# Gate columns inside wide products, bias rows on half the array, and a first block without lag in a four-layer hybrid network on one core

## The chip, the core and the metric

The kernel runs on one core of a Trainium2 chip. The metric is the device time of one execution in microseconds; before the change it is 2135.79 us, the median of three runs (2135.09 to 2136.02).

## What is computed

The reference sends one sequence of 256 positions, 1024 wide, through four layers. Each layer is a gated feed-forward block, a mixer and a second feed-forward block, each followed by a scaled residual and a layer norm. The mixers are, in order, a state-space mixer, attention with a forget gate ("fox"), attention over blocks ("moba", here one block, so plain causal attention), and a state-space mixer again. All is float32. Cut to what matters here:

```python
def mamba2_mixer(x, w_in, ...):
    zxbcdt = x @ w_in
    z, xbc, dt = jnp.split(zxbcdt, [SSM_D_INNER, SSM_D_INNER + SSM_CONV_DIM], axis=-1)
    ...
    dt = jax.nn.softplus(dt + dt_bias)

def fox_attention(x, w_in, b_f, w_out):
    q, k, v, f_logit = jnp.split(x @ w_in, [H * Dh, 2 * H * Dh, 3 * H * Dh], axis=-1)
    log_f = jax.nn.log_sigmoid(f_logit + b_f)
    cum = jnp.cumsum(log_f, axis=1)
    ...
    logits = einsum(qb, kb) * scale + (cq[..., :, None] - cum[..., None, :])
    p = jax.nn.softmax(jnp.where(kpos <= qpos, logits, -inf))
```

## The kernel before

The sequence is cut into two streams of 128 positions (`t` = 0 and 1), each a generator that receives one weight piece at a time. A piece is 1 MB: 128 partitions of 2048 columns. `fetch` loads it on SP's queue into one of three `raw` tiles; `load` splits it in four chunks into a high part `wh` (ScalarE, line 126) and the remainder `wl` (VectorE, line 127), five tiles each. Activations are split alike into `xh` and `xl` by `to_T`, after TensorE has transposed them (line 161, tile `tp`). Each product is three matmuls, `mm3` (lines 151 to 153): high by high, high by low, low by high. `proj512` covers half the contraction with a piece of 512 output columns, so two pieces make one bank; `proj256` covers all of it with 256 columns.

The planner at the end walks the blocks. Stream 0 takes piece `s`, then stream 1 takes piece `s - LAG`, with `LAG` = 2 and two pieces loaded ahead; at the end of a block stream 1 catches up. The tile scheduler then orders the instructions of each engine by priority and readiness; what is marked with `keep_in_program_order` stays where the code has it. PSUM has three pools of two banks: `T` (transposes, scores, small sums, tile `tp`), `G` (tile `gu`), and the accumulators (`acc`, `ga`).

The gates are separate. `small_w` loads and splits the 32 columns of dt (or the 16 of the forget gate) into the tile `dtw`, and `small_proj` (lines 324 to 334) multiplies them in 16 narrow matmuls per stream and layer. `log1p_exp` and the steps around it then turn them into log decays on VectorE; `stage_cum` sums them along the sequence with triangular matrices. In the fox layer `rows_T` (line 336) leaves the sums as rows, high parts on partitions 0 to 31 and low parts on 32 to 63, and `stage_s` adds each head's row to its scores with a full-array matmul whose moving operand is the 128 columns of one row tile and whose stationary operand is one column of the tile `sel` (line 649). A score block `stage_s` handles four heads of one stream: for each of two banks `Sv[0]`, `Sv[1]`, both from `T`, a mask product (line 644, tile `mlo`), the bias products, and then the score products on 64 partitions (line 655), which alternate between the two halves of the array in the code. Exponentials follow on ScalarE (line 663). The feed-forward activations are turned through DRAM by POOL's queue (lines 245 and 249, tiles `turn` and `aT`).

At the start, `init` loads stream 0's input, the first piece follows in four loads, then stream 1's input.

Of the kernel before, what the change touches and what calls it, by code (L numbers as in the profile page):

```python
# [7 lines left out]
F32 = mybir.dt.float32  # L8
# [7 lines left out]
D = 1024  # L16
# [23 lines left out]

SSM_ORDER = ["X0", "Z0", "X1", "Z1", "O0", "X2", "Z2", "X3", "O1", "Z3",
             "O2", "O3"]
ATT_ORDER = ["V0", "Q0", "V1", "Q1", "V2", "Q2", "V3", "Q3", "O0", "O1", "O2", "O3"]

# [5 lines left out]
def build(tc, x, wst, ln_g, ln_b, sm_dt, sm_rows, sm_conv, sm_nw, fx_f, fx_b, out, plan=None):  # L50
# [11 lines left out]
    if plan is None:  # L62
        plan = []
        for l in range(DEPTH):
            plan += [("ffn", l, 3 * l), ("mix", l, 3 * l + 1), ("ffn", l, 3 * l + 2)]

# [15 lines left out]
    nc.vector.memset(mhalf, -0.5)  # L82

    K = {}

    def consts():
# [13 lines left out]
        K["sel"] = cpool.tile([128, 32], FR, name="sel")  # L100
        nc.vector.tensor_add(K["sel"], ident[:, 0:32], ident[:, 32:64])
# [35 lines left out]
    def load(i, raw=None, pin=False):  # L137
# [20 lines left out]
    def transposes(src, n):  # L158
        tp = T()
        for j in range(n):  # L160
            nc.tensor.transpose(tp[:, j * 128:(j + 1) * 128], src[:, j * 128:(j + 1) * 128], ident)  # L161
        return tp

    def to_T(st, h):
        xh = spool.tile([128, KT, 128], FR, name=f"xh{st.t}", bufs=1)
        xl = spool.tile([128, KT, 128], FR, name=f"xl{st.t}", bufs=1)
        for half in range(2):
            tp = transposes(h[:, half * 512:half * 512 + 512], 4)
            sl = slice(half * 4, half * 4 + 4)
            split(tp.rearrange("p (a b) -> p a b", a=4), xh[:, sl], xl[:, sl])  # L170
# [153 lines left out]
    def small_proj(st, w, n, bias):  # L324

        ps = G()
        for k in range(KT):
            nc.tensor.matmul(ps[:, :2 * n], st.xh[:, k], w[:, k], start=k == 0, stop=False, skip_group_check=True)
            nc.tensor.matmul(ps[:, :n], st.xl[:, k], w[:, k, 0:n], start=False, stop=k == KT - 1,
                             skip_group_check=True)  # L330
        v = small()
        nc.vector.tensor_add(v[:, :n], ps[:, :n], bias)
        nc.vector.tensor_add(v[:, :n], v[:, :n], ps[:, n:2 * n])
        return v[:, :n]

# [10 lines left out]
    def sel(j):  # L346
        return bc(K["sel"][:, j:j + 1], 128)

    def small_w(src, n):
        raw = tmp(KT * n, "t1", 5)  # L350
        nc.sync.dma_start(raw, src)
        w = spool.tile([128, KT, 2 * n], FR, name="dtw", bufs=1)
        rv = raw.rearrange("p (k n) -> p k n", k=KT)
        split(rv, w[:, :, 0:n], w[:, :, n:2 * n])
        return w
# [6 lines left out]
    def ssm_small(j):  # L362
# [4 lines left out]
        s.dt = small_w(sm_dt[j], 32)  # L367
        s.rows = tmp(96, "rows", 1)
        nc.sync.dma_start(s.rows, bc(sm_rows[j:j + 1, :], 96))
# [3 lines left out]
        nc.scalar.activation(s.na, s.rows[:, 32:64], AF.Exp)  # L373
# [12 lines left out]
    def ssm(st, j):  # L386
# [4 lines left out]
        def stage_dt():  # L391
            v = small_proj(st, s.dt, 32, s.rows[:, :32])
# [49 lines left out]
        def stage_x(g):  # L442
            if t == 0:
                s.xb[g] = spool.tile([128, 6, S + 3], F32, name="xb", tag="t4", bufs=2)
                s.cv[g] = spool.tile([128, 6, S], F32, name="cv", tag="t4", bufs=2)
                nc.gpsimd.memset(s.xb[g][:, :, 0:3], 0.0)
            xc = tmp(512, "t2", 4)
            nc.scalar.activation(xc, bank.pop(g), AF.Copy)
            tp = transposes(xc, 4)
            nc.vector.tensor_copy(s.xb[g][:, 0:4, 3 + t * 128:131 + t * 128], tp.rearrange("p (a b) -> p a b", a=4))  # L450
# [3 lines left out]
        def stage_bc(g):  # L454
            bcs = tmp(256, "t1", 5)
            nc.scalar.activation(bcs, bank.pop(g)[:, :256], AF.Copy)
# [470 lines left out]
```

## Time and profile before

| | |
|---|---|
| median of three runs | 2135.79 us |
| profiled execution | 2134.62 us |
| its span | 2132.7 us |
| TensorE busy | 2108.4 us, 99% |
| VectorE, ScalarE, POOL busy | 69%, 55%, 22% |
| HBM traffic | 205 GB/s over the span |

A row of the timeline, as below, gives a start in us from the span's beginning, a duration, the engine, the line of the kernel, the operation, the output and input tiles and a count; a bracket tells the idle time before the instruction on its engine and what ended it. A matmul's duration contains its way through the array, which overlaps the next one, so the distance from start to start is what it takes of TensorE.

### The profile page before, as it was taken

How to read it: one execution, taken by the hardware profiler on the slowest of the kernel's cores; microseconds unless marked ns; L12 is line 12 of the kernel's file. 1: busy time of each engine (PE TensorE's matmuls, PEld its weight loads, DVE VectorE, ACT ScalarE, POOL GpSimd, SP SyncE). 2: the span in 40 equal slices, each digit the busy share in tenths (PEclk: the TensorE clock that was granted, in tenths of full speed). 3: DMA queues.
4: the chain of work that ended last, by engine and by line, in shares of the span. 5: the costliest groups of instructions: out<-in, count | busy, mean ns of one | idle time of the engine just before them, and what ended most of it. 6: DMA issues, size and time to landing. Idle time of an engine off the chain costs nothing.

```text
span 2132.7 us, 29860 instructions
## 1 busy us (share of the span) xinstructions
PE 2108.4 (99%) x10346; PEld 1745.6 (82%) x10346; DVE 1464.4 (69%) x2833; ACT 1172.6 (55%) x2446; POOL 474.0 (22%) x858
## 2 busy tenths in 40 slices
PE   8999999999999999999999999999999999999998
PEld 7888888888888888788888887788888888888886
DVE  6657888756766575755675575666575678898655
ACT  6445996544444555544544455544444448975442
POOL 2431000233143200043233300033323310002331
PEclk9999999999999999999999999999999999999999
DMA  9665554666576643466666653376666655546662
GB/s 318 226 228 200 179 197 160 225 230 224 199 254 227 222 159 119 155 233 222 221 226 231 229 200 131 129 247 219 225 225 232 223 198 201 179 167 217 232 228 94
DMA packets 225927, 438.81 MB, mean 206 GB/s; under 512 B 20464, under 2 KB 20976, under 8 KB 225776
## 3 DMA queue, kind: packets, MB, share of 16 engines
q1 hardware_dynamic: 197616, 394.92, 51.8%
q0 software_dynamic: 28160, 41.99, 6.6%
q8 instruction: 81, 1.33, 0.3%
q14 instruction: 70, 0.57, 0.1%
HBM read 414.74 MB, written 22.09 MB: 205 GB/s over the span
## 4 chain that ended last, share of the span: by engine, by line
PE 94%; DVE 2%; ACT 2%; DMA 1%; issue 1%; SPq 0%; POOL 0%; DVEq 0%; ACTq 0%
PE gu L151 16%; PE gu L153 16%; PE gu L152 16%; PE acc L153 9%; PE acc L151 9%; PE acc L152 9%; PE ga L151 4%; PE ga L152 4%; PE ga L153 4%; PE tp L161 3%; PE gu L513 1%; DVE wl L127 1%; PE gu L698 1%; ACT wh L126 1%; DMA raw<-in_w_dram 0%
## 5 line engine op out<-in xcount | busy, mean ns | idle before, releaser
L127 DVE TENSOR_TENSOR wl<-raw,wh 128x512 fp32r<-128x512 f32 x1408 | 887.5, 683 | 375.9 <-ACT wh L126 374.1
L126 ACT ACTIVATE wh<-raw 128x512 fp32r<-128x512 f32 x1408 | 776.4, 621 | 504.2 <-PE gu L153 225.0
L151 PE MATMUL gu<-wh,xh 128*128 128x512 f32 (+1 forms) x1600 | 618.9, 387 | 1.3 <-ACT t L522 1.2
L152 PE MATMUL gu<-wl,xh 128*128 128x512 f32 (+1 forms) x1600 | 617.9, 386 | 0.0
L153 PE MATMUL gu<-wh,xl 128*128 128x512 f32 (+1 forms) x1600 | 617.6, 386 | 0.0
L249 POOL DMA_DIRECT2D aT<-turn x640 | 348.3, 551 | 489.5 <-issue 301.1
L151 PE MATMUL acc<-wh,ah 128*128 128x512 f32 x896 | 352.8, 394 | 0.0
L153 PE MATMUL acc<-wh,al 128*128 128x512 f32 x896 | 352.3, 393 | 0.0
L151 PEld LDWEIGHTS gu<-wh,xh 128*128 128x128 f32 x1600 | 301.1, 188 | 62.3 <-ACT t L522 1.6
L152 PE MATMUL acc<-wl,ah 128*128 128x512 f32 x896 | 351.3, 392 | 0.0
L152 PEld LDWEIGHTS gu<-wl,xh 128*128 128x128 f32 x1600 | 301.1, 188 | 59.7 <-issue 0.5
L153 PEld LDWEIGHTS gu<-wh,xl 128*128 128x128 f32 x1600 | 300.9, 188 | 59.5 <-DVE xl L127 0.3
L273 ACT ACTIVATE t<-gu 128x256 f32<-128x256 f32 x176 | 67.5, 383 | 268.4 <-PE gu L153 247.8
L275 DVE TENSOR_TENSOR t<-t,gu 128x256 f32<-128x256 f32 x176 | 73.6, 418 | 193.3 <-ACT t L273 193.3
L153 PEld LDWEIGHTS acc<-wh,al 128*128 128x128 f32 x896 | 168.3, 188 | 36.3 <-DVE al L127 2.5
L151 PEld LDWEIGHTS acc<-wh,ah 128*128 128x128 f32 x896 | 168.3, 188 | 35.9 <-issue 1.5
L152 PEld LDWEIGHTS acc<-wl,ah 128*128 128x128 f32 x896 | 168.3, 188 | 34.5 <-issue 1.3
L245 POOL DMA_DIRECT2D turn<-tb x160 | 90.3, 565 | 328.3 <-DVE tb L243 305.0
L151 PE MATMUL ga<-wh,xh 128*128 128x512 f32 (+1 forms) x448 | 159.8, 357 | 1.4 <-ACT xh L126 1.4
L153 PE MATMUL ga<-wh,xl 128*128 128x512 f32 (+1 forms) x448 | 155.9, 349 | 0.0
L152 PE MATMUL ga<-wl,xh 128*128 128x512 f32 (+1 forms) x448 | 155.7, 348 | 0.0
L193 POOL TENSOR_TENSOR rstd<-ve,mhalf 128x1 f32<-128x1 f32 x24 | 22.6, 942 | 485.1 <-DVE ve L191 485.1
(171 smaller groups left out, 1667.9 us busy)
## 6 DMA issues: line engine op xcount, KB each, us to landing
raw<-in_w_dram SPq DMA_DIRECT2D x351, 1024.0 KB, 5.3
turn<-tb POOLq DMA_DIRECT2D x160, 128.0 KB, 3.2
aT<-turn POOLq DMA_DIRECT2D x640, 32.0 KB, 4.0
mt<-cums SPq DMA_DIRECT2D x32, 256.0 KB, 4.5
gb<-in_ln_g_dram SPq DMA_DIRECT2D x12, 512.0 KB, 4.8
gb<-in_ln_b_dram SPq DMA_DIRECT2D x12, 512.0 KB, 5.9
nw<-in_sm_nw_dram SPq DMA_DIRECT2D x8, 256.0 KB, 5.6
h<-in_x_dram SPq DMA_DIRECT2D x4, 256.0 KB, 4.2
```

Of the source, the lines that this page charges most:

```text
L126: a = nc.scalar.activation(wh, raw, AF.Copy)
L127: return a, nc.vector.tensor_sub(wl, raw, wh.bitcast(F32))
L151: nc.tensor.matmul(o, xh, wh, start=start, stop=False)
L152: nc.tensor.matmul(o, xh, wl, start=False, stop=False)
L153: nc.tensor.matmul(o, xl, wh, start=False, stop=stop)
L161: nc.tensor.transpose(tp[:, j * 128:(j + 1) * 128], src[:, j * 128:(j + 1) * 128], ident)
L193: nc.gpsimd.tensor_tensor(rstd, ve, mhalf, op=ALU.pow)
L245: nc.gpsimd.dma_start(dr, b.rearrange("p q k t -> p (q k t)"))
L249: nc.gpsimd.dma_start(aT[32 * q:32 * q + 32].rearrange("p i k t -> p i (k t)"), dv[q])
L273: nc.scalar.activation(sg, gu[:, :256], AF.Silu)
L275: nc.vector.tensor_mul(a, sg, gu[:, 256:])
L513: ins = nc.tensor.matmul(y[:, c64], mt[h // 4][:, h % 4], xd[:, c64], start=True, stop=True)
```

## The change

Four edits come together.

1. The dt columns join the first group's products: group 0's x, b and c columns and the 32 of dt (800 in all) become two banks of 416 and 384 columns in four pieces, which are padded to 2048 columns in memory and split only where they are filled (`cols`, `step`). The fox layer's 16 gate columns join the first value piece: 272 columns in two pieces. `small_w` and `small_proj` go. The order of stages in group 0 of the state-space layer follows: b, c and dt come with the first bank, x with the second.
2. The fox bias rows are written to DRAM and read back as a tile `biases` (`s.R`) of two halves of 64 partitions, by POOL's queue (`bias_rows`). One matmul on 64 partitions then adds the rows of one bank. The second score bank comes from `G`, and the first bias and score products keep their place.
3. The first scores of the fox layer come two pieces later (`wait`).
4. In the first block stream 1 runs without lag up to piece 6, with a lag of one up to 9, then two. Until piece 4 the TensorE products, transposes and splits keep the code's order (`opening`). A dummy SiLU stands at the start of ScalarE's work.

```diff
+        cols = [1664, 1664, 1536, 1536] if it == "X0" else [2048] * (3 if k == "X" else 2)
...
+        cols = [1088, 1088] if fox and it == "V0" else [2048] * (2 if k == "Q" else 1)
...
+    warm = cpool.tile([128, 1], F32, name="warm")
+    nc.scalar.activation(warm, mhalf, AF.Silu)
...
-        for c in range(0, 2048, 512):
-            sl = slice(c, c + 512)
+        step = cols[i] // (-(-cols[i] // 544))
+        for c in range(0, cols[i], step):
+            sl = slice(c, c + step)
...
+    opening = []
+
     def mm3(o, xh, xl, wh, wl, start, stop):
-        nc.tensor.matmul(o, xh, wh, start=start, stop=False)
+        first = nc.tensor.matmul(o, xh, wh, start=start, stop=False)
+        if opening:
+            tc.keep_in_program_order(first)
...
-    def proj512(st, ps, half, w):
+    def proj512(st, ps, half, w, n=512):
         wh, wl = w
         for kk in range(4):
             k = half * 4 + kk
-            mm3(ps, st.xh[:, k], st.xl[:, k], wh[:, kk * 512:(kk + 1) * 512], wl[:, kk * 512:(kk + 1) * 512],
+            mm3(ps[:, :n], st.xh[:, k], st.xl[:, k], wh[:, kk * n:(kk + 1) * n], wl[:, kk * n:(kk + 1) * n],
                 k == 0, k == KT - 1)
...
-    def small_proj(st, w, n, bias):
...
+    def bias_rows(c, dst):
+
+        dr = dpool.tile([2, 16, 128], FR, name="fbias", bufs=3)
+        for p in range(2):
+            nc.gpsimd.dma_start(dr[p], c[32 * p:32 * p + 16])
+        for b in range(2):
+            nc.gpsimd.dma_start(dst[64 * b:64 * b + 8], dr.rearrange("p (g i b) k -> b (p g) i k", g=4, i=2)[b])
...
         def stage_dt():
-            v = small_proj(st, s.dt, 32, s.rows[:, :32])
+            v = small()
+            nc.vector.tensor_add(v, bank["b"][:, 384:416], s.rows[:, :32])
...
         at(where["X", 0, 1], stage_dt)
-        at(where["X", 0, 2] + 1 - t, stage_cum)
+        at(where["X", 0, 3] + 1 - t, stage_cum)
         for g in range(N_GRP):
-            b = where["X", g, 2]
-            at(b - 1, stage_x, g)
-            at(b, stage_bc, g)
+            b = where["X", g, 2 if g else 3]
+            at(b - 1 if g else b, stage_x, g)
+            at(b if g else 1, stage_bc, g)
...
             def stage_cum():
-                d.rows = rows_T(d.h, d.l, K["ntri"], f"rowsT{t}")
+                own = rows_T(d.h, d.l, K["ntri"], "rowsT")
                 if t == 0:
-                    s.toend = rows_T(d.h, d.l, K["strict"], "rowsTe")
+                    R = spool.tile([128, 2, 384], FR, name="biases", tag="t4", bufs=2)
+                    nc.gpsimd.memset(R.bitcast(F32), 0.0)
+                    s.R = [R[:, :, 0:128], R[:, :, 128:384]]
+                    bias_rows(own, s.R[0])
+                    bias_rows(rows_T(d.h, d.l, K["strict"], "rowsTe"), s.R[1][:, :, 0:128])
+                else:
+                    bias_rows(own, s.R[1][:, :, 128:256])
...
-            Sv = [T()[:, :2 * nk].rearrange("p (h k) -> p h k", h=2) for b in range(2)]
+            Sv = [f()[:, :2 * nk].rearrange("p (h k) -> p h k", h=2) for f in (T, G)]
...
-                if fox:
-                    for i in range(2):
-                        for kt, off, rows in parts:
-                            nc.tensor.matmul(Sv[b][:, i, off:off + 128], sel(g * 4 + 2 * i + b), rows, start=False,
-                                             stop=True, skip_group_check=True)
+            halves = [slice(64 * b, 64 * b + 64) for b in range(2)]
+            if fox:
+                for b, half in enumerate(halves):
+                    ins = nc.tensor.matmul(Sv[b], K["sel"][half, g:g + 1].to_broadcast([64, 128]), s.R[t][half],
+                                           start=False, stop=True, skip_group_check=True)
+                    if b == 0:
+                        tc.keep_in_program_order(ins)
...
-            at(where["Q", 0, 0], stage_f)
-            at(where["Q", 0, 1] + 1, stage_cum)
+            at(where["V", 0, 1], stage_f)
+            at(where["Q", 0, 1], stage_cum)
...
+            wait = 2 if fox and g == 0 else 0
+            at(q + 1 + wait, stage_s, g)
...
+    def lag_at(s):
+
+        return LAG if s > 9 else 1 if s > 6 else 0
...
+        for s in range(base, base + n):
+            if s:
+                advance(0, s)
...
+            while second <= s - lag_at(s):
+                advance(1, second)
+                second += 1
```

On TensorE the program begins as follows before the change (`h_85` is stream 0's input, `h_119` stream 1's):

```order
L161 MATMUL tp<-ident,h_85 128x128 x8
L161 MATMUL tp<-ident,h_119 128x128 x3
L151 MATMUL gu<-wh,xh_93 128x512
L161 MATMUL tp<-ident,h_119 128x128 x5
L152 MATMUL gu<-wl,xh_93 128x512
```

In the changed kernel (`h_87` and `h_95`) it begins so, and after twelve products of stream 0 goes on as the second piece shows:

```order
L199 MATMUL tp<-ident,h_87 128x128 x8
L187 MATMUL gu<-wh,xh_98 128x512
L190 MATMUL gu<-wl,xh_98 128x512
L191 MATMUL gu<-wh,xl_99 128x512
L187 MATMUL gu<-wh,xh_98 128x512
```

```order
L190 MATMUL gu<-wl,xh_98 128x512
L191 MATMUL gu<-wh,xl_99 128x512
L199 MATMUL tp<-ident,h_95 128x128 x8
L187 MATMUL gu<-wh,xh_137 128x512
L190 MATMUL gu<-wl,xh_137 128x512
```

Stream 1's transposes have moved behind stream 0's first piece, and stream 1 takes that piece next, where it came third before.

In the first state-space layer, TensorE before the change ends stream 0's first two x pieces and takes the gate's narrow products (`dtw`; the first two of 16 and the last are in these two pieces), then the gate's transposes (`t_1925`):

```order
L151 MATMUL ga<-wh,xh_1816 128x512
L152 MATMUL ga<-wl,xh_1816 128x512
L153 MATMUL ga<-wh,xl_1817 128x512
L328 MATMUL gu<-dtw,xh_1816 128x64
L329 MATMUL gu<-dtw,xl_1817 128x32
```

```order
L329 MATMUL gu<-dtw,xl_1817 128x32
L161 MATMUL tp<-ident,t_1925 128x128 x4
L151 MATMUL ga<-wh,xh_1816 128x256
L152 MATMUL ga<-wl,xh_1816 128x256
L153 MATMUL ga<-wh,xl_1817 128x256
```

In the changed kernel the first bank is followed by the second at once, and stream 1's transposes (`h_1795`) follow the ninth product of its second piece:

```order
L187 MATMUL ga<-wh,xh_1813 128x416
L190 MATMUL ga<-wl,xh_1813 128x416
L191 MATMUL ga<-wh,xl_1814 128x416
L187 MATMUL ga<-wh,xh_1813 128x384
L190 MATMUL ga<-wl,xh_1813 128x384
L191 MATMUL ga<-wh,xl_1814 128x384
```

```order
L191 MATMUL ga<-wh,xl_1814 128x384
L199 MATMUL tp<-ident,t_1902 128x128
L199 MATMUL tp<-ident,h_1795 128x128 x4
L199 MATMUL tp<-ident,t_1902 128x128 x2
L187 MATMUL ga<-wh,xh_1813 128x384
```

The narrow products are gone, and less work of stream 0 stands ahead of stream 1's transposes.

A score block of stream 0 in the fox layer, on TensorE before the change (the third group; `tp` are the two banks):

```order
L644 MATMUL tp<-idb,mlo 128x256
L649 MATMUL tp<-rowsT_7449,sel 128x128 x2
L644 LDWEIGHTS mlo
L644 MATMUL tp<-idb,mlo 128x256
L649 MATMUL tp<-rowsT_7449,sel 128x128 x2
L655 MATMUL tp<-xdt_7765,qT 128x128 x4
L151 MATMUL ga<-wh,xh_7365 128x512
```

and in the changed kernel:

```order
L690 MATMUL tp<-idb,mlo 128x256
L690 LDWEIGHTS mlo
L690 MATMUL gu<-idb,mlo 128x256
L695 MATMUL tp<-biases,sel 128x256
L695 MATMUL gu<-biases,sel 128x256
L702 MATMUL tp<-xdt_7680,qT 128x128
L702 MATMUL gu<-xdt_7680,qT 128x128
L702 MATMUL tp<-xdt_7680,qT 128x128
L702 MATMUL gu<-xdt_7680,qT 128x128
L190 MATMUL ga<-wl,xh_7283 128x512
```

Two bias products take the place of four, and the second bank is a `gu`.

## Rows read from the trace of the kernel before

**Rows 1.** The page: busy time of the engines, the granted clock in 40 slices, and the chain that ended last by engine.

```profile
PE 2108.4 (99%) x10346; PEld 1745.6 (82%) x10346; DVE 1464.4 (69%) x2833; ACT 1172.6 (55%) x2446; POOL 474.0 (22%) x858
...
PEclk9999999999999999999999999999999999999999
...
PE 94%; DVE 2%; ACT 2%; DMA 1%; issue 1%; SPq 0%; POOL 0%; DVEq 0%; ACTq 0%
```

**Rows 2.** The waits of TensorE: what waited for what, us in total, how often, the longest.

```profile
PE tp L644 <- ACT mt L663: 2.6, 6, 0.6
...
PE tp L649 <- DVE rowsT L343: 0.4, 1, 0.4
PE tp L644 <- DVE rowsT L343: 0.4, 1, 0.4
```

**Rows 3.** The timeline of TensorE in two stretches of products, 512 and 256 columns wide.

```profile
21.49 0.40 PE L151 MATMUL gu<-wh,xh 128*128 128x512 f32 x1
...
28.30 0.39 PE L151 MATMUL gu<-wh,xh 128*128 128x512 f32 x1
...
773.14 0.28 PE L151 MATMUL ga<-wh,xh 128*128 128x256 f32 x1
...
775.18 0.28 PE L153 MATMUL ga<-wh,xl 128*128 128x256 f32 x1
```

**Rows 4.** The timeline of TensorE at the gate projection of stream 0 in the first state-space layer: its first narrow product, and what follows the sixteenth.

```profile
199.36 0.19 PE L328 MATMUL gu<-dtw,xh 128*128 128x64 f32 x1
...
201.06 0.33 PE L161 MATMUL tp<-ident,t 128*128 128x128 f32 x1
```

**Rows 5.** The timeline of TensorE at four score blocks of the fox layer: stream 0's first, the product ahead of it, and the one after it; stream 0's second; stream 1's second; stream 0's third.

```profile
775.97 0.40 PE L152 MATMUL ga<-wl,xh 128*128 128x512 f32 x1
776.77 0.27 PE L644 MATMUL tp<-idb,mlo 128*128 128x256 bf16 x1 [0.40 <-DVE rowsT L343]
...
777.44 0.72 PE L655 MATMUL tp<-xdt,qT 64*128 64x128 f32 x8
778.09 0.50 PE L153 MATMUL ga<-wh,xl 128*128 128x512 f32 x1
...
802.08 0.27 PE L644 MATMUL tp<-idb,mlo 128*128 128x256 bf16 x1
...
803.48 0.71 PE L655 MATMUL tp<-xe,qT 64*128 64x128 f32 x4
804.12 0.50 PE L151 MATMUL ga<-wh,xh 128*128 128x512 f32 x1
...
823.09 0.28 PE L644 MATMUL tp<-idb,mlo 128*128 128x256 bf16 x1
...
825.31 0.39 PE L151 MATMUL ga<-wh,xh 128*128 128x256 f32 x1
...
828.54 0.27 PE L644 MATMUL tp<-idb,mlo 128*128 128x256 bf16 x1
...
830.47 0.50 PE L151 MATMUL ga<-wh,xh 128*128 128x512 f32 x1
```

**Rows 6.** The same for three score blocks of the moba layer, which has no biases: stream 0's first, stream 1's first, stream 0's last.

```profile
1273.86 0.39 PE L644 MATMUL tp<-idb,mlo 128*128 128x256 bf16 x2
...
1274.83 0.50 PE L151 MATMUL ga<-wh,xh 128*128 128x512 f32 x1
...
1291.12 0.39 PE L644 MATMUL tp<-idb,mlo 128*128 128x256 bf16 x2
...
1292.54 0.39 PE L151 MATMUL ga<-wh,xh 128*128 128x256 f32 x1
...
1345.23 0.28 PE L644 MATMUL tp<-idb,mlo 128*128 128x256 bf16 x1
1346.12 0.27 PE L644 MATMUL tp<-idb,mlo 128*128 128x256 bf16 x1 [0.61 <-ACT mt L663]
...
1346.97 0.50 PE L151 MATMUL ga<-wh,xh 128*128 128x512 f32 x1
```

**Rows 7.** The page's DMA issues: KB each, median us from issue to landing, on POOL's queue, and the busy time and mean of their issue on POOL.

```profile
turn<-tb POOLq DMA_DIRECT2D x160, 128.0 KB, 3.2
aT<-turn POOLq DMA_DIRECT2D x640, 32.0 KB, 4.0
...
L249 POOL DMA_DIRECT2D aT<-turn x640 | 348.3, 551 | 489.5 <-issue 301.1
```

**Rows 8.** The timeline at the openings of two mixers: a table load of ScalarE in the first state-space layer, and stream 1's first product in the fox layer.

```profile
203.72 1.28 ACT L307 ACT_TABLE_LOAD   x1
...
768.89 0.38 PE L151 MATMUL ga<-wh,xh 128*128 128x256 f32 x1 [1.02 <-ACT xh L126]
```

**Rows 9.** The timeline of TensorE at the start.

```profile
9.08 0.87 PE L161 MATMUL tp<-ident,h 128*128 128x128 f32 x3 [3.48 <-DVE wl L127]
9.60 0.78 PE L151 MATMUL gu<-wh,xh 128*128 128x512 f32 x1
...
12.10 0.63 PE L151 MATMUL gu<-wh,xh 128*128 128x512 f32 x1
...
12.95 0.63 PE L153 MATMUL gu<-wh,xl 128*128 128x512 f32 x1
```

**Rows 10.** ScalarE and VectorE there: the first chunks of the first piece.

```profile
6.12 1.20 ACT L126 ACTIVATE wh<-raw 128x512 fp32r<-128x512 f32 x2
...
6.87 2.78 DVE L127 TENSOR_TENSOR wl<-raw,wh 128x512 fp32r<-128x512 f32 x4
```

More of the change, by code (lines that the diff above doesn't have):

```diff
@@ L43, with ssm_pieces, att_pieces, sub_cols @@
 ATT_ORDER = ["V0", "Q0", "V1", "Q1", "V2", "Q2", "V3", "Q3", "O0", "O1", "O2", "O3"]
+def ssm_pieces():
+    out = []
+    for it in SSM_ORDER:
+        k, g = it[0], int(it[1])
+        cols = [1664, 1664, 1536, 1536] if it == "X0" else [2048] * (3 if k == "X" else 2)
+        out += [(k, g, n, c) for n, c in enumerate(cols)]
+    return out
+def att_pieces(fox):
+    out = []
+    for it in ATT_ORDER:
+        k, g = it[0], int(it[1])
+        cols = [1088, 1088] if fox and it == "V0" else [2048] * (2 if k == "Q" else 1)
+        out += [(k, g, n, c) for n, c in enumerate(cols)]
+    return out
+def sub_cols(kind, layer):
+    if kind == "ffn":
+        return [2048] * 3 * NC_F
+    mk = mixer_of(layer)[0]
+    return [p[3] for p in (ssm_pieces() if mk == "ssm" else att_pieces(mk == "fox"))]
 def mixer_of(layer):
     return ("ssm", "fox", "moba")[layer % 3], layer // 3
-def build(tc, x, wst, ln_g, ln_b, sm_dt, sm_rows, sm_conv, sm_nw, fx_f, fx_b, out, plan=None):
+def build(tc, x, wst, ln_g, ln_b, sm_rows, sm_conv, sm_nw, fx_b, out, plan=None):
     nc = tc.nc
@@ L160, in transposes @@
         for j in range(n):
[L161 removed]
+            ins = nc.tensor.transpose(tp[:, j * 128:(j + 1) * 128], src[:, j * 128:(j + 1) * 128], ident)
+            if opening:
+                tc.keep_in_program_order(ins)
         return tp
@@ L169, in to_T @@
             sl = slice(half * 4, half * 4 + 4)
-            split(tp.rearrange("p (a b) -> p a b", a=4), xh[:, sl], xl[:, sl])
+            for ins in split(tp.rearrange("p (a b) -> p a b", a=4), xh[:, sl], xl[:, sl]):
+                if opening:
+                    tc.keep_in_program_order(ins)
         st.xh, st.xl = xh, xl
@@ L322, in log1p_exp @@
         return q
-    def small_proj(st, w, n, bias):
[L326 to L334, printed above, removed]
     def rows_T(h, l, mat, tag):
@@ L600, in stage_f @@
             def stage_f():
-                v = small_proj(st, s.f, 16, s.rows)
-                q = log1p_exp(v, 16)
+                v = small()
+                nc.vector.tensor_add(v[:, :16], bank["v", 0][:, 256:272], s.rows)
+                q = log1p_exp(v[:, :16], 16)
                 m = small()
-                nc.vector.tensor_scalar_min(m[:, :16], v, 0.0)
+                nc.vector.tensor_scalar_min(m[:, :16], v[:, :16], 0.0)
                 lf = small()
@@ L722, in attn @@
             at(q, stage_q, g)
-            at(q + 1, stage_s, g)
-            at(where["V", g, 0], stage_v, g)
-            at(q + 2, att, g)
+            wait = 2 if fox and g == 0 else 0
+            at(q + 1 + wait, stage_s, g)
+            at(where["V", g, int(fox and g == 0)], stage_v, g)
+            at(q + 2 + wait, att, g)
         first_o = where["O", 0, 0]
@@ L774, in build @@
     sts = [St(), St()]
-    W = {}
+    W, loaded = {}, [0]
     def advance(t, i):
         if t == 0:
-            for k in range(max(W, default=-1) + 1, min(i + PF, NP - 1) + 1):
-                W[k] = load(k)
+            while len(loaded) <= min(i + PF, NP - 1):
+                k = len(loaded)
+                loaded.append(k)
+                W[k] = load(k, pin=k == 1)
         try:
@@ L790, in build @@
     raw0 = fetch(0)
+    next(gens[1])
     next(gens[0])
     W[0] = load(0, raw0, pin=True)
+    opening.append(True)
+    gens[0].send(W[0])
     next(gens[1])
[L794 removed]
+    base = second = 0
     for kind, l, li in plan:
[L796 to L802 removed]
+        n = len(sub_cols(kind, l))
+        for s in range(base, base + n):
+            if s:
+                advance(0, s)
+            if s == 4:
+                opening.clear()
                 ln_weights(plan[0][2])
[L804 to L805 removed]
+            while second <= s - lag_at(s):
+                advance(1, second)
+                second += 1
         base += n
+        while second < base:
+            advance(1, second)
+            second += 1
     ctx.close()
@@ L816, in cols512 @@
 def cols512(a):
-    return list(a.reshape(2, 4, 128, 512).transpose(0, 2, 1, 3).reshape(2, 128, 2048))
+    P = np.zeros((2, 128, 2048), a.dtype)
+    n = a.shape[1]
+    P[:, :, :4 * n] = a.reshape(2, 4, 128, n).transpose(0, 2, 1, 3).reshape(2, 128, 4 * n)
+    return list(P)
 def cols256(a):
@@ L864, in pack_att @@
     return P
-def pack_small(w):
-    return np.ascontiguousarray(w.reshape(w.shape[0], KT, 128, -1).transpose(0, 2, 1, 3).reshape(w.shape[0], 128, -1))
 def layout(I, plan=None):
```

103 lines of the change are left out of this document (52 added, 51 removed).

## The prediction

> **What bounds the kernel now.** I read the page first: TensorE is busy 99% of the 2132.7 us span, the chain that ended last is 94% TensorE, and the granted clock stands at full speed in all forty slices [rows 1]. Every microsecond that leaves TensorE's queue therefore leaves the time, as long as the others keep up; VectorE (69%) and ScalarE (55%) count only where TensorE waits for them. Past the start its recorded waits are short: 2.6 us in six places at the attention scores, 0.4 us twice at bias rows [rows 2]. The "busy" of a matmul overlaps its neighbour, so I take prices from starts in the timeline. From 21.49 to 28.30 us are 30 steps of 512 columns, 6.81 / 30 = 0.227 us each; of 256 columns 17 steps from 773.14 to 775.18, 0.120 us each [rows 3]. A column more costs 0.107 / 256 = 0.42 ns.
>
> **Term A, dt and forget gates.** One separate projection is 16 narrow matmuls; the first starts at 199.36 and what follows them at 201.06: 1.70 us, or 0.106 us for a product 32 or 64 columns wide [rows 4]. Two state-space layers and one forgetting layer with two streams each have six calls: 6 x 1.70 = 10.2 us go. Their columns now ride in wide products whose number stays 48 per state-space stream (24 of 416 and 24 of 384 columns for 24 of 512 and 24 of 256): 32 columns more x 24 x 0.42 ns = 0.32 us, four times 1.28 us. In the forgetting layer 16 columns more in 24 products: 0.16 us, twice 0.32. A = -10.2 + 1.6 = -8.6 us, on the path throughout, good to half a microsecond. The three extra loads (one in each of these layers) are 1 MB of padded columns each in a stage where the DMA queues are not the wait; I cost them at nothing, hidden by the two-piece prefetch. Without that cover each could cost one TensorE piece of about 3 us.
>
> **Term B, biases as half-array products.** A score block of the forgetting layer runs from its first mask product to the product after it. For stream 0 I read 1.32, 2.04 and 1.93 us (the fourth like the last), for stream 1 2.22 [rows 5]: 1.32 + 2.04 + 2 x 1.93 + 4 x 2.22 = 16.1 us. The layer without biases does the same masks and scores in 0.97 and 1.42 us [rows 6]. To that the change adds one pair on the two halves of the array: 256 columns for stream 0, 512 for stream 1. Pairs on different halves do overlap: eight score records in alternating order take the 0.65 us from 777.44 to 778.09, and four on one half take the 0.64 us from 803.48 to 804.12 [rows 5]. So a pair costs one product, 0.12 or 0.23 us: 4 x (0.97 + 0.12) + 4 x (1.42 + 0.23) = 11.0 us. B = -5.1 us. If the pairs did not overlap, 4 x (0.12 + 0.23) = 1.4 us of it stay; one of the sixteen blocks is still issued out of alternation, some 0.3 us. Ends -5.5 and -3.5.
>
> **Term C, the second score bank.** Three blocks of the bias-free layer wait between the two mask products, as from 1345.23 to 1346.12, a block of 1.74 where 0.97 would do [rows 6]; the 2.6 us of [rows 2] are these three and three inside the forgetting layer, counted in B. The second bank now comes from the other pool, so the wait on the previous exponentials goes. Next late is that pool's own last user, the value product's split. Ends 0 and -2.0 (three times up to 0.77); I take -1.5.
>
> **Term D, reaching the first biases.** Now the queue loses time at the first block of each stream, both released by VectorE's bias rows with 0.4 us of recorded wait [rows 2]. From start to start the first of them is 775.97 to 776.77 where 0.23 would do, 0.57 us [rows 5]; the other taken alike, 1.1 us. These go, since the first scores come later. But the rows now pass through DRAM on POOL's queue: four writes, then the reads. From the transposed gates I count 0.7 us for ScalarE's and VectorE's copies, two issues and the landing of the second own write (its neighbours take 3.2 us on that queue and 0.55 us an issue), two more issues and a landing of 4.0 [rows 7]: 0.7 + 1.1 + 3.2 + 1.1 + 4.0 = 10.1 us. In the changed order TensorE has 30 products of 512 columns and ten 128-wide ones before it needs them: 6.8 + 1.1 = 7.9 us. Stall 2.2 us; the rows are 8 KB where the measured ones are 32 and 128 KB, so I take 1.0, ends 0 and 5. Behind that instruction waits all of TensorE, and behind TensorE the release of weight buffers. D = -0.1 us. The second stream has over 20 us and does not wait.
> The Trainium skill, "DMA: Bandwidth & Descriptors", section on the anatomy of a POOL-issued DMA, puts the fixed cost of one at about 2.0 us, most of it the write receipt. By that estimate the hops take 0.7 + 1.1 + 2.0 + 1.1 + 2.0 = 6.9 us, no stall, and the sum would be 1.0 us lower; the rows above are longer, and no row here has a POOL transfer this small.
>
> **Term E, the openings of the mixers.** The 1.70 us of narrow products also filled time in which the second stream's normalised rows were not ready. In the state-space layer a table load of 1.28 us stands on ScalarE shortly before the second stream's split [rows 8]. In the changed order TensorE reaches these transposes some 4 us earlier; the input is there, but the transpose bank must be freed by a VectorE copy behind three weight splits, and ScalarE has the gate's absolute value and that table load first. I work out waits of 0.25 and 0.5 us, so +0.7 for each of two layers. In the forgetting layer the second stream already waits 1.02 us [rows 8], and its transposes now come earlier in the queue: 0. E = +1.4, ends -1 and +5, the upper one if ScalarE's two extra table loads per layer (1.28 us each) both reach TensorE.
>
> **Term F, the first block without lag.** Today TensorE transposes both inputs before it starts: idle until 9.08, first product at 9.60, then products 0.43 us apart (12.10 to 12.95 is two) until the pace doubles after 12.95 [rows 9]. 512 columns in 0.43 us is the 1.2 GHz level; the clock column does not show it. In the change the first product needs only the first chunk's high part, ready at 6.12 + 0.60 (half of 1.20), and the low part at 6.87 + 0.69 (a quarter of 2.78) [rows 10]: 12 products from 7.6 at 0.43 end near 12.3; four transposes, the split's 0.6 us and 0.3 of hops bring the second stream in at 13.7, its low half costs 0.3 more, 14.0. By 21.49 that gives 12 + 7.5 / 0.227 = 45 products. Before, it was 36 of stream 0 (pieces 0 to 2) and three of stream 1, 39. 6 x 0.227 = 1.4 us gained. F = -1.4; the next late thing is the evacuation of the first gate bank, some 0.3 us ahead of its user, so it cannot be much more than -1.9. The other end is +1.0.
> What keeps the half pace is the risk: the transposes and the wait for the split now stand in the middle of the opening. The Trainium skill, "TensorE: Matmul & The Clock Gate", Part 4 (PE-mode transpose), says that transposes do not count as activity towards full clock the way matmuls do. By that the second stream's 12 products would still run at 0.43, 2.4 us lost, and F would be +1.0. In these rows the pace doubled after transposes and matmuls mixed, so the trace does not decide it.
>
> **Sum.** -8.6 - 5.1 - 1.5 - 0.1 + 1.4 - 1.4 = -15.3 us against the profiled execution's 2134.62 us (its span and 1.9 us around it), which is 1.2 us under the median of the runs, 2135.79. Against the median: **2120.5 us**, 0.7% faster.
>
> **Rivals.**
> *The state-space layers give it back.* ScalarE and VectorE are dense there, the first group's x columns come one piece later, the convolution with them, and the two table loads are added. For: the table loads and the longer split list. Against: weights lie ready several microseconds early and few recorded waits point there [rows 2]. Price: E at +5 and 2 us later in each layer: 2120.5 + 3.6 + 4 = 2128.
> *The attention saving is not TensorE's.* If softmax sets the pace of the two attention layers, B and C return as waits elsewhere: 2120.5 + 6.6 = 2127. Against: TensorE's waits on exponentials are 2.6 us in all.
> *The opening stays at half pace*, the page's rule, as a mechanism of this kernel: twelve more products at 0.43 instead of 0.227: 2120.5 + 2.4 = 2122.9.
> *Slower than before: the bias rows come late.* One mechanism, the DRAM round trip ahead of the first scores. It decides from a hop of about 10 us: 0.7 + 1.1 + 10 + 1.1 + 10 = 22.9, less 7.9 is a stall of 15 us, where I have 1.0; then 2134.5, and with products at half pace after such a pause 20 x 0.2 = 4 us more, 2138.5. For: it is a chain of two transfers on one queue that TensorE waits for in order. Against: 3.2 and 4.0 us measured [rows 7].
> *The change doesn't do what it says*: halves that do not overlap, +1.4 us, 2121.9. Inside the forecast.
>
> **From cases to numbers.** Forecast with its near variants (the halves, a smaller or larger C and F: 2115 to 2124.5) 0.66, the half pace in the opening 0.08, state-space layers 0.13, attention 0.09, late bias rows 0.04. The ends of the terms add to about 2114 (F -1.9, B -5.5, C -2, D -1.1, E -1) on one side; the state-space case sets 2129 on the other. Range 2114 to 2129. A measurement of this kernel tells about 0.2%, 4.3 us, from no change. Faster by more than that needs under 2131.5: 0.92. Within: 0.05, the upper tails of the two give-back cases. Slower: 0.03, most of the late bias rows.
>
> **What would show it.** In the changed profile: no products on the narrow gate weights, and 416, 384 and 272 columns at 0.19, 0.17 and 0.13 us between starts (A). Score blocks of 1.1 and 1.65 us, bias pairs a few ns apart (B). No wait between the two mask products (C). A wait of TensorE on the bias tile's DMA at the first block, under 2 us (D). Waits of under 1 us at each mixer's second-stream transposes (E). A first product near 7 us and the 45th near 21.5 us (F). I am wrong if TensorE waits over 3 us in one place inside a mixer, if waits on ScalarE or VectorE grow by more than 5 us in all, or if the opening's pace doubles later than 15 us.

## The result, and the profile after

The changed kernel takes 2125.19 us, the median of four runs (2123.60 to 2126.55), against 2135.90 for the kernel before in the same comparison: a ratio of 0.9950, interval 0.9933 to 0.9967. That is 10.7 us faster, where 15.3 were forecast (2120.5; the range 2114 to 2129 holds it). The profiled execution took 2124.81 us, 9.8 under the one before. A second set of five runs of the same kernel gave 2123.79 (ratio 0.9948, 0.9935 to 0.9962).

The page of the changed kernel, the lines that answer to [rows 1]:

```profile
PE 2099.0 (99%) x10218; PEld 1735.6 (82%) x10218; DVE 1461.4 (69%) x2829; ACT 1177.0 (55%) x2453; POOL 480.9 (23%) x871
...
PEclk9999999999999999999999999999999999999999
...
PE 91%; DVE 4%; ACT 2%; DMA 1%; issue 1%; POOL 0%; SPq 0%; DVEq 0%; ACTq 0%
```

TensorE is as full as before, but 3% of the chain has gone from it to VectorE (2% to 4%) and others (in the profile of the second set TensorE has 93%). Its waits (us in total, how often, the longest) answer to [rows 2]:

```profile
PE tp L518 <- ACT cv L464: 2.3, 2, 1.2
PE gu L527 <- DVE t L521: 2.1, 2, 1.1
PE gu L187 <- ACT wh L159: 1.2, 1, 1.2
...
PE tp L199 <- ACT t L492: 1.0, 1, 1.0
```

The 2.6 us on the exponentials and the two waits on the bias rows are gone. New are the first two rows and the fourth, all in the state-space layers: L518 multiplies b and c after the convolution (tile `cv`), L527 uses that product (tile `t`), and L199 there transposes x columns that ScalarE has copied (L492). Where the time went shows best from block to block. The second stream's norm has one POOL instruction on the tile `rstd`; the distances between its starts in the two profiles give this table (us), beside what the forecast's terms make for the same stretch:

| stretch | before | after | difference | forecast |
|---|---|---|---|---|
| start to the first norm | 197.7 | 197.8 | +0.1 | -1.4 (F) |
| first state-space layer | 197.8 | 198.8 | +1.0 | -2.1 (A -2.76, E +0.7) |
| forgetting layer | 137.0 | 127.4 | -9.6 | -8.3 (A -3.1, B -5.1, D -0.1) |
| bias-free layer | 125.4 | 123.4 | -1.9 | -1.5 (C) |
| second state-space layer | 197.7 | 197.6 | -0.1 | -2.1 |

The rest, the feed-forward blocks, is 0.8 us longer in all. The attention layers gave more than forecast, the state-space layers nothing.

A score block of the changed kernel, stream 0's third, in the timeline of TensorE (start, duration, ...):

```profile
823.07 0.28 PE L690 MATMUL tp<-idb,mlo 128*128 128x256 bf16 x1
823.19 0.27 PE L690 MATMUL gu<-idb,mlo 128*128 128x256 bf16 x1
823.40 0.38 PE L695 MATMUL tp<-biases,sel 64*128 64x256 f32 x1
823.40 0.38 PE L695 MATMUL gu<-biases,sel 64*128 64x256 f32 x1
823.62 0.27 PE L702 MATMUL tp<-xdt,qT 64*128 64x128 f32 x1
...
824.15 0.50 PE L190 MATMUL ga<-wl,xh 128*128 128x512 f32 x1
```

The two bias products start together and the scores follow 0.22 us later. The block takes 1.08 us, where [rows 5] had 1.93, and 0.11 more than the 0.97 of a block without biases [rows 6]: a pair costs one product.

The place in the first state-space layer where the time is lost, the second group's convolution results on TensorE, in the kernel before

```profile
254.13 0.60 PE L161 MATMUL tp<-ident,t 128*128 128x128 f32 x4
...
271.08 0.49 PE L481 MATMUL tp<-cv 128*128 128x128 f32 x2
271.32 0.48 PE L153 MATMUL ga<-wh,xl 128*128 128x512 f32 x1
```

and in the changed one:

```profile
256.11 0.60 PE L199 MATMUL tp<-ident,t 128*128 128x128 f32 x4
...
273.61 0.49 PE L518 MATMUL tp<-cv 128*128 128x128 f32 x2 [1.16 <-ACT cv L464]
...
276.25 1.12 PE L527 MATMUL gu<-xe,t 128*128 128x512 f32 x2 [1.05 <-DVE t L521]
```

The first row of each is the transpose of the group's x columns, with which its convolution begins. TensorE waits twice, 2.2 us together: for ScalarE's SiLU on the convolution (L464), then for VectorE's step on the product of b and c (L521). Both layers show the same two waits.

Which side moved can be read in the second state-space layer, which has no late weights; it starts (the norm's POOL instruction) at 1750.20 us before the change

```profile
1821.52 1.28 ACT L437 ACT_TABLE_LOAD   x1
1822.81 0.63 ACT L437 ACTIVATE cv<-cv 128x512 f32<-128x512 f32 x1
...
1823.50 0.49 PE L481 MATMUL tp<-cv 128*128 128x128 f32 x2
```

and at 1740.48 after it:

```profile
1811.19 1.28 ACT L541 ACT_TABLE_LOAD   x1
1812.48 0.63 ACT L541 ACTIVATE mt<-mt 128x512 f32<-128x512 f32 x1
1813.13 1.28 ACT L464 ACT_TABLE_LOAD   x1
1814.43 0.63 ACT L464 ACTIVATE cv<-cv 128x512 f32<-128x512 f32 x1
```

Counted from the layer's start, the SiLU ended at 73.24 us before and TensorE came at 73.30, a tie. In the changed kernel TensorE is free at 73.45, so it is no earlier by the clock; it has twelve products on `acc` behind it (one piece, 2.7 us) that stood behind this place before. The SiLU begins 1.3 us later, at 73.95 in place of 72.61: x is transposed at 51.80 in place of 51.09, VectorE ends the convolution 0.4 us later, and ScalarE takes an exponential with its table load ahead of the SiLU (the first two rows), which it had done some 3 us sooner before.

### The profile page after: what moved, and what is told of

Its sections match the earlier page's. It is cut to its first block, busy times and chain, and to the rows that moved or that the text cites. A ratio compares the mean times of both kernels' runs of the same rounds, so it can differ in the third digit from the quotient of the medians.

```text
span 2122.9 us, 29645 instructions
## 1 busy us (share of the span) xinstructions
PE 2099.0 (99%) x10218; PEld 1735.6 (82%) x10218; DVE 1461.4 (69%) x2829; ACT 1177.0 (55%) x2453; POOL 480.9 (23%) x871
## 4 chain that ended last, share of the span: by engine, by line
PE 91%; DVE 4%; ACT 2%; DMA 1%; issue 1%; POOL 0%; SPq 0%; DVEq 0%; ACTq 0%
PE gu L187 16%; PE gu L190 16%; PE gu L191 16%; PE acc L191 9%; PE acc L187 9%; PE acc L190 9%; PE ga L187 3%; PE ga L190 3%; PE ga L191 3%; PE tp L199 3%; DVE wl L160 2%; PE gu L550 1%; DMA raw<-in_w_dram 1%; PE gu L747 1%; DVE cv L461 1%
## 5 line engine op out<-in xcount | busy, mean ns | idle before, releaser
L160 DVE TENSOR_TENSOR wl<-raw,wh 128x512 fp32r<-128x512 f32 (+1 forms) x1412 | 889.1, 680 | 363.1 <-ACT wh L159 361.7
L159 ACT ACTIVATE wh<-raw 128x512 fp32r<-128x512 f32 (+1 forms) x1412 | 778.8, 620 | 511.2 <-PE gu L191 230.0
L187 PE MATMUL ga<-wh,xh 128*128 128x512 f32 (+4 forms) x448 | 159.5, 357 | 0.4 <-ACT xh L159 0.4
L190 PE MATMUL ga<-wl,xh 128*128 128x512 f32 (+4 forms) x448 | 156.8, 351 | 0.0
L191 PE MATMUL ga<-wh,xl 128*128 128x512 f32 (+4 forms) x448 | 155.7, 349 | 0.0
```

The costliest lines, as they stand in the source:

```text
L159: a = nc.scalar.activation(wh, raw, AF.Copy)
L160: return a, nc.vector.tensor_sub(wl, raw, wh.bitcast(F32))
L187: first = nc.tensor.matmul(o, xh, wh, start=start, stop=False)
L190: nc.tensor.matmul(o, xh, wl, start=False, stop=False)
L191: nc.tensor.matmul(o, xl, wh, start=False, stop=stop)
```

## The experiments

The theory after this reading (G, give-back): before the change TensorE came to that place just as ScalarE and VectorE were done with the convolution; what it now saves ahead of it goes into later products, and comes back there as a wait. Three runs test it, and two more with a part of the computation left out.

**The gate columns of the state-space layers undone.** dt gets its own weights and narrow products again in these two layers, and x, b and c their old order; the forgetting layer keeps its change.

```diff
-        cols = [1664, 1664, 1536, 1536] if it == "X0" else [2048] * (3 if k == "X" else 2)
+        cols = [2048] * (3 if k == "X" else 2)
...
-            nc.vector.tensor_add(v, bank["b"][:, 384:416], s.rows[:, :32])
+            v = small_proj(st, s.dt, 32, s.rows[:, :32])
```

> The changed kernel with edit 1 undone in the two state-space layers alone (separate dt weights, 16 narrow products, the old order of x, b and c); all else as changed. Theory G (give-back): in these layers ScalarE and VectorE set the pace at the second group's convolution, so what TensorE saves before it comes back as a wait. The traces show the two mixers 1.0 us longer and 0.1 us shorter with the change, so this kernel is 0.9 us faster than the changed one: 2124.3 us, between 2123.5 and 2125.2, each mixer again 197.8 us. The forecast's own sizing (A at 2.76 us a layer, E at 0.7 us a layer given back): 4.1 us slower, 2129.3 us.

Measured: 2123.82 us (2123.44 to 2124.07), ratio 0.9940 (0.9927 to 0.9954), as G says; the two mixers take 197.8 and 197.7 us, and the waits on cv and t are absent. Under its own kernel before it lies 12.5 us, where the two sets of the changed kernel lie 10.7 and 11.2 under theirs. So this half of edit 1 brings nothing or costs up to 1.8 us. As load and order were undone together, it doesn't tell them apart.

**The consumers of the second group's convolution one piece later.**

```diff
-            c = b + (LAG if t == 0 else 0)
+            c = b + (LAG if t == 0 else 0) + int(g == 1)
```

> The changed kernel with everything that uses the second group's convolution (stage_back and what follows it) one piece later in both streams. Theory G: the convolution's results come about 2.4 us late for TensorE, and a piece of 2.7 us per stream put ahead covers it, so the waits on cv and t (1.2 and 1.1 us in each state-space layer) go: 2120.6 us, between 2119.5 and 2122.5. Rival S (saturation): ScalarE and VectorE have no slack anywhere in the layer, the wait only moves to the next consumer: 2124.5 to 2126.

Measured: 2120.80 us (2120.34 to 2122.17), ratio 0.9927 (0.9915 to 0.9940). The waits on cv and t are gone; what is left there is smaller:

```profile
PE tp L199 <- ACT t L480: 2.2, 2, 1.1
PE gu L187 <- ACT t L559: 1.3, 2, 0.7
...
PE tp L695 <- DMA biases<-fbias: 0.4, 1, 0.4
```

The mixers take 197.0 and 196.2 us. It is the fastest complete kernel here, 4.4 us under the first set of the changed kernel and 3.0 under the second (by the ratios 4.9 and 4.5 us).

**The same shift in the kernel before**, the control:

> The control to e2: the kernel before with the same shift (what uses the second group's convolution comes one piece later). Theory G: before the change TensorE reaches that place just as the convolution is done (recorded waits there under 0.1 us, longest step from start to start 0.41 us), so the shift has little to give: 0.3 to 1 us faster, 2135.0 us, between 2134 and 2136.5. Rival: the shift is worth its 4.4 us in any kernel and has nothing to do with the dt columns: 2131 to 2132.5.

Measured: 2136.01 us, ratio 1.0002 (0.9993 to 1.0011). The shift alone is worth nothing. It helps only where TensorE waits at that place, as G has it.

**Less convolution in both kernels.** Two of the three earlier taps are left out (`range(1, 4)` becomes `range(3, 4)` in `conv`).

> The kernel before, without two of the three earlier taps of the convolution in all groups (that part of the computation is left out): 12 VectorE operations of 0.4 us less in each of eight group convolutions. To be read beside the changed kernel with the same cut. Alone: the kernel before waits little there, so 2133 to 2136 us by both theories.

> The changed kernel without the same two taps. Theory G: with VectorE's convolution 4.8 us shorter per group the waits on cv and t (2.3 us a layer) go, and the state-space layers keep what TensorE saves: 14.5 to 16.5 us under the kernel before with the same cut. Rival P (placement): the loss comes from the order of instructions (x of the first group one piece later, table loads), not from VectorE's load; then the distance stays 9.5 to 11.5 us.

Measured: 2135.11 us for the kernel before with this cut (ratio 0.9994, 0.9986 to 1.0003), 2117.87 for the changed one (0.9915, 0.9902 to 0.9929): 17.2 us apart in place of 10.7. That is more than the 14.5 to 16.5 expected. Between the profiles of these two the first state-space layer is 1.6 us shorter (197.6 to 196.0) and the second 2.8 (197.6 to 194.8), which is the 2.76 us of term A in full; the first keeps a wait of 1.1 us on another row (L492). So with VectorE relieved TensorE's saving reaches the end. The kernel before gained nothing from the same relief. (The first block, which the cut does not touch, happens to differ by 3.3 us between these two profiles.) Rival P's 9.5 to 11.5 is out, but its mechanism is not: a shorter convolution also covers a later start of it.

**The clock behind these waits.** The nine runs of the changed kernel lie between 2122.24 and 2126.55 us, the five without the waits (gate columns undone) within 0.7 us. The mean granted clock goes with it: of the nine runs the three at 0.998 take 2124.58, 2126.39 and 2126.55 us, the six at 0.999 take 2122.24 to 2125.57, and the five have 0.999 throughout. These waits are not the only source: 21 runs of the kernel before, some at 0.998 too, spread over 3.2 us (2135.16 to 2138.33). The profile of the second set shows where the clock goes:

> The changed kernel itself, on the same chip as e9 and e10. No theory changes it: 2125.2 us, between 2124.2 and 2126.2; its profile shows again 2.3 us of waits on cv and t in each state-space layer, and the late load of about 1.5 us on ScalarE in the first one alone.

Measured: 2123.79 us (2122.24 to 2126.39), a little under the range expected. Busy time by stretch in the second state-space layer (PE, PEld, DVE, ACT, POOL, then the granted clock, the DMA share and GB/s), first in the profile of the first set, then in that of the second:

```profile
1815.00:1820.00 5.00, 3.83 (x18) 2.76 (x19) 4.75 (x9) 4.97 (x11) 0.00 (x0) 1.00 0.40 152
```

```profile
1815.00:1820.00 5.00, 3.99 (x9) 2.55 (x10) 5.00 (x10) 4.97 (x8) 0.00 (x0) 0.66 0.32 120
```

The timeline of TensorE in the profile of the second set, ahead of and in that stretch:

```profile
1813.37 0.49 PE L518 MATMUL tp<-cv 128*128 128x128 f32 x2 [1.17 <-ACT cv L464]
...
1816.01 2.07 PE L527 MATMUL gu<-xe,t 128*128 128x512 f32 x2 [1.05 <-DVE t L521]
...
1818.31 0.63 PE L190 MATMUL gu<-wl,xh 128*128 128x512 f32 x1
1818.73 0.58 PE L191 MATMUL gu<-wh,xl 128*128 128x512 f32 x1
```

The same two waits stand in both. In one execution the clock stays full, in the other it is granted at 0.66 over these 5 us, the products go 0.42 us apart (1.2 GHz) until 1819.15, and this layer takes 199.1 us, where the first layer of this profile takes 197.9 and the second one of the first profile 197.6, both with the two waits and the clock full. So the waits of 2.2 us here cost 2.2 or some 3.4 to 3.7. Six profiles have the two waits in both layers: the two of the changed kernel and those of the experiments below with the lag of 2, the transposes in the middle, the scores at the old place and one pool for the banks. The clock falls behind these waits in four of the twelve layers.

**Late weights.** In the first profile ScalarE waits 1.6 us for a weight piece in the first state-space layer, and TensorE 1.0 us behind it (the row L492 above). Is it the padded fourth piece? The kernel with the shift, loading only the columns in use:

```diff
-        for k in range(0, 4, n):
-            nc.sync.dma_start(rv[:, k:k + n], wst[i][k:k + n].rearrange("a p c -> p a c"))
+        full, part = divmod(cols[i], 512)
+        for k in range(0, full, n):
+            m = min(full, k + n)
+            nc.sync.dma_start(rv[:, k:m], wst[i][k:m].rearrange("a p c -> p a c"))
+        if part:
+            nc.sync.dma_start(rv[:, full, :part], wst[i][full][:, :part])
```

> The kernel of e2_late_group1 with the padded columns no longer loaded (1664, 1536 and 1088 of 2048 columns are fetched, by one short transfer more where they are no multiple of 512). Theory W (weights): the fourth piece of 1 MB in the first group makes a weight load late in the first state-space layer (ScalarE waits 1.2 to 2.2 us on it in every profile with the change, never without), which costs TensorE 0.6 us there in e2; less to load takes this away: 2120.1 us, between 2119.3 and 2120.8. Rival: the load is late by its issue or by other traffic: 2120.8 us and the same wait.

Measured: 2122.10 us (2120.62 to 2122.52), ratio 0.9938 (0.9926 to 0.9951), no gain, and ScalarE's wait in that layer is still there (TensorE's behind it is 0.8 us):

```profile
ACT wh L159 <- DMA raw<-in_w_dram: 1.3, 1, 1.3
```

The time alone can't price the padding, since in this profile the clock fell as well (granted 0.66 from 285 to 290 us, behind a wait of 1.1 us on ScalarE), which the profile of the kernel with the shift does not have; the wait decides. In the second profile of the changed kernel, with the padding, it is absent. So theory W falls: the bytes of the padding are not the cause, and not every execution has the late load. But TensorE's wait behind it (0.6 to 1.6 us) is in eight of the ten profiles with a fourth piece in the first group, and in none of the four with three, so the extra load itself stays the suspect. It was not tested by itself.

**The opening.** Edit 4 undone, once in the changed kernel and once in the kernel with the shift and the short loads:

```diff
-    return LAG if s > 9 else 1 if s > 6 else 0
+    return LAG
...
-    opening.append(True)
```

> The changed kernel with edit 4 undone (lag 2 from the start, no pinned order, no dummy SiLU). By the traces' product counts (product 60 at 26.44 us after, 26.26 before) the new opening gives nothing: 2125.2 us, within 0.7. By the forecast's term F: 1.4 us slower, 2126.6.

> The kernel of e9_late1_trim with edit 4 undone. Product 60 came at 26.26, 26.68 and 27.53 us in the three profiles with the old opening and at 25.18 to 26.44 us in those with the new one, 1.2 us earlier on the mean. Theory (term F of the forecast right): 1.2 to 1.5 us slower than e9, some 2121.4 us. Rival (the first pair of profiles, 0.1 us): as fast as e9.

Measured: 2126.52 us (2123.63 to 2128.93) against 2125.19 and 2123.79 with the new opening; then 2121.30 (2120.83 to 2122.85) against 2122.10. The times differ both ways, by less than they scatter. The profiles say more. Over the five with lag 2 (before and four experiments) the 45th product starts at 22.6 to 23.9 us, over the eight with the new opening at 20.5 to 22.4, 1.5 us earlier on the mean, and the second stream's norm at the end of the block 1.0 us earlier (197.4 against 198.4). The two ranges of the norm overlap (196.0 to 198.3 and 197.7 to 199.3). The first pair of profiles, with its +0.1, had a late one of the new kind.

The second stream's transposes in the middle of the first piece:

```diff
+            if kk == 2 and halfway:
+                halfway.pop()()
...
     opening.append(True)
+    halfway.append(lambda: next(gens[1]))
     gens[0].send(W[0])
-    next(gens[1])
```

> The changed kernel with the second stream's transposes in the middle of the first piece (after six of its twelve products) and not behind it. Theory: of the 2.1 us between the first piece's last product and the second stream's first, 0.7 us are waiting for the split and its hops, which six products then cover: 2124.5 us, between 2124.0 and 2125.0. Rival (clock): the half pace lasts as long as the first transposes and splits do, and what is saved there is lost to slower products: 2125.2 to 2126.

Measured: 2127.50 us, but from 2124.16 to 2131.77. The 24th product comes at 15.7 us, where the first profile of the changed kernel has 17.6 and the other seven with the new opening 15.7 to 17.3. Later in the block the profile has ScalarE waiting 16.0 us in all on weights and TensorE waiting 3.4 us between 80 and 100 us. Inconclusive.

**The bias rows' round trip.** The first scores at the old place (`wait = 0`):

> The changed kernel with the forgetting layer's first scores at the old place (two pieces earlier). Theory: the bias rows need the round trip through DRAM, whose last read lands about 9.5 us after the sums; TensorE needs them two pieces (about 5.5 us of TensorE work) earlier and waits about 5 us once: 2130 us, between 2128 and 2132. Rival: other work is pulled ahead of the waiting instruction, and little is lost: 2125 to 2127.

Measured: 2133.26 us (2130.93 to 2136.05), ratio 0.9985 (0.9976 to 0.9993): 8 us of the 10.7 are gone, more than expected, and the clock falls here too:

```profile
786.09 0.35 PE L695 MATMUL tp<-biases,sel 64*128 64x256 f32 x1 [2.37 <-DMA biases<-fbias]
786.37 0.65 PE L190 MATMUL ga<-wl,xh 128*128 128x512 f32 x1
786.82 0.63 PE L191 MATMUL ga<-wh,xl 128*128 128x512 f32 x1
```

```profile
785.00:790.00 5.00, 3.91 (x15) 2.75 (x16) 1.70 (x4) 0.00 (x0) 0.63 (x2) 0.66 0.50 168
```

The wait of 2.4 us ends at 786.09; behind it products stand 0.45 us apart and the granted clock is 0.66. The second stream's first block waits on its bias rows too, 1.2 us at 802.96, with the clock again at 0.66 over the 5 us from 803. The forgetting layer takes 134.9 us in this profile, 7.5 more than with the scores two pieces later; the second state-space layer, with its two waits and a fall of the clock of its own, takes 200.6.

**Both score banks from one pool** (`for f in (T, T)`):

> The changed kernel with both score banks from the pool T again. Theory: the waits between the two mask products come back, in the bias-free layer 2.0 us, in the forgetting layer 1 to 1.5 us: 2128.5 us, between 2127.5 and 2129.5. Rival: the exponentials' order is what makes the waits go, not the pool: 2125.2.

Measured: 2128.16 us (2125.63 to 2130.98), ratio 0.9960 (0.9946 to 0.9973). The bias-free layer is back at 125.4 us, the forgetting layer at 128.5, and the wait returns:

```profile
PE tp L690 <- ACT mt L712: 1.9, 4, 0.6
```

## Why the prediction was right, and where it was off

- **The range holds, partly by luck.** The state-space layers took back 5.0 us of the forecast and the first block of the first profile 1.5; the feed-forward blocks are 0.8 longer, and the attention layers gave 1.7 more. The upper end, 2129, came from the first rival, which is the one that happened in part. The lower end was added up wrongly: the ends named give 2115.7, not 2114.
- **Term A was right in the forgetting layer and, as TensorE time, in the state-space layers**, where with a lighter convolution 2.8 us of it arrive in the second. Its three extra loads were put at nothing; in the first of these layers TensorE waits 1.0 us behind a late weight piece (L492), which only kernels with the fourth piece show.
- **Term E is the step that failed.** It took TensorE's early arrival to cost 0.7 us a layer at the second stream's transposes. There it cost little (0.13 us); the wait came some 70 us later, at the second group's convolution, and A's 2.76 us were lost: 3.7 us in the first layer, 3.2 of them recorded as waits with the late weights, 2.7 in the second, 2.2 recorded. The first rival had the mechanism, state-space layers that give it back through ScalarE, VectorE and the convolution, and 2128 us for it; but it expected the first group's convolution, and 7.6 us in the two layers where 5.0 were measured (+0.9 against the -4.1 forecast). What I read as slack, "few recorded waits point there" [rows 2], was a tie (the SiLU done 0.06 us before TensorE comes): an engine that arrives just in time records no wait. Whether the engines' load or the order on them (x's transposes behind more products, the exponential ahead of the SiLU) weighs more was not separated; a run with the new columns and the old order would.
- **Term B had the price of a block right**: 1.08 and 1.64 us measured, 1.09 and 1.65 forecast. The halves overlap. Together the eight take 11.8 us, not 11.0, since one block of stream 1 is issued out of alternation (in two parts, 1.08 and 1.53 us), 1.0 us over the others, and I had allowed 0.3 for it as one end: 4.4 us saved of 5.1.
- **Term C**: 1.9 us in the bias-free layer, near the far end of its bound, where I took 1.5; undoing it costs 2.0 us there and 1.1 in the other layer.
- **Term D was 1.0 us too dear.** The approach stalls went, and TensorE waits 0.0 us on the bias rows (0.4 in one experiment). The round trip was about as long as I made it, 9.5 us from the sums (777.15) to the landing of the second read (786.65), where I had 10.1; but TensorE needs 9.2 us to get from there to the block (777.15 to 786.38), where I counted 7.9 by ideal steps, and comes to the bias products at 786.70. Its issues in the changed kernel:

```profile
biases<-fbias POOLq DMA_DIRECT2D x6, 8.0 KB, 2.5
fbias<-rowsT POOLq DMA_DIRECT2D x4, 8.0 KB, 2.4
fbias<-rowsTe POOLq DMA_DIRECT2D x2, 8.0 KB, 3.5
```

Small transfers land in 2.4 to 3.5 us, over the 2.0 us of the Trainium skill ("DMA: Bandwidth & Descriptors", anatomy of a POOL-issued DMA), and two of the three rows under the 3.2 to 4.0 of [rows 7]; by the estimate from that page (6.9 us) there would have been slack of two microseconds, and the trace shows 0.05 us between the landing and the product. The run with the scores at the old place shows the slower-side rival's mechanism, with the half pace behind the stall that it named.
- **The forgetting layer's opening**: E took 0 for it; the 1.02 us wait of [rows 8] went as well. With the four terms, -3.1 - 4.4 - 1.1 - 1.0 = -9.6, the measured -9.6 is accounted for.
- **Term F** shows as 1.5 us at the 45th product and 1.0 at the end of the block over the profiles, 1.4 forecast; the times do not resolve it. The half-pace rival did not happen: behind the eight transposes the second stream's products soon run 0.23 us apart, the 2.4 GHz level. The split behind them came later than I put it, 14.71 and not 14.0 in the first profile.

```profile
6.96 0.80 PE L187 MATMUL gu<-wh,xh 128*128 128x512 f32 x1 [1.20 <-ACT wh L159]
...
13.01 1.45 PE L199 MATMUL tp<-ident,h 128*128 128x128 f32 x8
14.71 0.50 PE L187 MATMUL gu<-wh,xh 128*128 128x512 f32 x1 [0.25 <-ACT xh L159]
...
15.77 0.39 PE L187 MATMUL gu<-wh,xh 128*128 128x512 f32 x1
16.00 0.40 PE L190 MATMUL gu<-wl,xh 128*128 128x512 f32 x1
```

## What to carry to other kernels

Time taken from an engine that is 99% busy is worth something only up to the next place where it meets another engine's chain; an absence of waits there can mean slack or a tie, and moving the consumer later in the old kernel and in the new tells which (here 0 and 3 to 5 us). Compare when both sides arrive, by the clock: here TensorE came no earlier, it came with more work done, and the other chain came later. A shortcut for TensorE may need its consumers set later in the order, as the one-piece shift did here. One profile against one profile is good to a microsecond per block at best: the opening's gain showed only over a dozen.

## What the runs showed of the hardware

Two waits of 1.2 and 1.05 us, 2.6 us apart from start to start, leave the granted clock at 1.00 in one execution and at 0.66 over the 5 us around the second in another. It fell in four of the twelve layers that show these waits, and one such layer took 1.2 to 1.5 us more (199.1 against 197.6 and 197.9), so short waits can widen the scatter as well as the time. Two matmuls on the two halves of the array, of 256 columns each, start in the same 0.01 us, and the next pair follows after 0.22 us.
